# Hybrid transformer block: the down, attention-output and second-block output products as one 512-column and one 256-column matmul for each chunk of K

## The chip, the cores and the metric

The kernel runs on one core of one Trainium2 chip. Its metric is the device time of one execution in microseconds (us); lower is better. The kernel before was timed three times: 1444.11, 1445.13 and 1448.83 us, median 1445.13 us.

## The reference

The program is two blocks of two layers each, on 256 tokens (in the second block also 256 context tokens), width D = 1024, all in float32. The lines whose products the change touches are these:

```python
# first block, both layers
merged = gates[:, :, 0] * y_a + gates[:, :, 1] * y_b + gates[:, :, 2] * y_c
x = x + merged @ w_o                                  # 1024 x 1024
h = rmsnorm(x, norm_mlp)
return x + jnp.square(jax.nn.relu(h @ w_up)) @ w_down # 1024 x 4096, then 4096 x 1024
# second block, both layers: x (in its first layer also the context) gets
x = x + gate * (y @ w_out)                            # 1024 x 1024
```

The rest (the projections into queries, keys, values and gates, five kinds of attention and a long convolution, the norms) is as before.

## The kernel before, in words

**Layout.** Activations stand transposed: 128 features on the partitions, 256 tokens along the free dimension, so an activation of width 1024 is 8 chunks of 128x256. Weights come in tiles of 128x1024: for one block of 128 output features, 8 chunks of 128 input features.

**Precision.** Every large product is made of exact parts. A value v is split into hi, its rounding to the matmul's format (a copy on ScalarE, L291 for weights, L275 for activations), and lo = v - hi (a subtraction on VectorE, L292 and L276). For each chunk of K, `mm3` issues three matmuls into one accumulation: high weights by high activations (L332), high weights by low activations (L333), low weights by high activations (L334). The parts of an activation chunk lie side by side in one 128x512 tile (`pair`), except those of the MLP's hidden layer, which were two 128x512 tiles `uh` and `ul` for two chunks each. An output of 128 features by 256 tokens fills half of a PSUM bank (2 KB, 512 float32 columns).

**Weights.** `weights` loads a tile by a DMA on SyncE's queue into one of 5 raw buffers, and splits it into one of 3 hi and 3 lo buffers. So the hi copy of a tile waits until TensorE has finished the tile three before it, and TensorE has two tiles of work left when the copy starts.

**The first block's layer** ends with three stages: the output stage (8 outputs c of 64 matmul chunks in all, over the activations `mg`; VectorE adds each output to x[c], L753; `gx` makes the parts of the next stage's input h[c] from it, on ScalarE at L493 and on VectorE at L494; a square for the next norm goes to ScalarE, and is summed on GpSimd, L421), and two halves of the MLP, each an up stage (h times w_up, ReLU, square, split into u) and a down stage (16 chunks for each of 8 outputs; L785 multiplies by the norm's factor, L786 adds to x[c]). Between these, `fill` puts pieces of the second block that depend on nothing (conditioning products L840, spectra of the long convolution).

**The second block** has the same kind of output product three times: `project_out` for x and then for the context (8 outputs of 8 chunks; one VectorE operation for each output, L1154), and `project` in its last layer, in two halves of 8 outputs by 4 chunks (L1378), the very end of the program.

**Order.** The program is traced once, and a scheduler then sets the order of the instructions on each engine from the dependences and its own estimates. Each engine runs its list in order; waits between engines are semaphores. PSUM has three rotating banks for these products (`ps_mm`).

## Time and profile before

| | |
|---|---|
| runs | 1444.11, 1445.13, 1448.83 us |
| span of the profiled execution, first to last instruction | 1448.5 us |
| its own time | not listed apart from its span; of the three runs the slowest, 1448.83 us, lies 0.3 us above it |
| mean granted TensorE clock | 0.998 |
| TensorE matmuls | 1427.0 us busy, 99% of the span, 10528 of them |
| VectorE | 1048.7 us, 72% |
| ScalarE | 776.5 us, 54% |
| GpSimd | 108.4 us, 7% |
| DMA | 234.94 MB, 162 GB/s in the mean |

A matmul's recorded duration runs from its issue to the arrival of its last result, so consecutive matmuls overlap in the record; what one costs a stream of them is the distance between two starts. Busy times of VectorE overlap too, by some 0.08 us for each pair of instructions.

The stages that the change touches lie here (us from the span's start; the rows of their windows stand further below): first layer, output stage from 245.3 to 268.7, down stages from 320.8 to 374.5 and from 433.0 to 491.2; second layer, output stage from 724.5 to 748.0, down stages from 804.0 to 859.6 and from 912.0 to 959.2; second block, `project_out` for x from 1201.0 to 1224.6 and for the context from 1224.6 to 1248.5, `project` from 1420.9 to the end.

### The profile page before, as it was taken

To read this page: it belongs to the slowest core of one execution; us is meant where nothing else is said; L and a number is where in the kernel's file an instruction comes from. 1 tells how busy PE (TensorE), PEld (TensorE's weight loads), DVE (VectorE), ACT (ScalarE), POOL (GpSimd) and SP (SyncE) were. 2 spreads that over 40 slices of the span, in tenths; PEclk is the share of its full clock that TensorE was granted. 3 is DMA by queue.
4 is the path that set the end of the run, shared out by engine and by line. 5 is a ranking of instruction groups with operands and counts; after the bars stand their busy time and mean duration, and the time that the engine had idled before them with its cause. 6 is when DMAs were issued, how large, how long until landed. Compare 5 with 4: busy or idle time off the path is not lost. (4 is left out here: it accounts for less than half of the span.)

```text
span 1448.5 us, 26508 instructions
## 1 busy us (share of the span) xinstructions
PE 1427.0 (99%) x10528; PEld 1284.2 (89%) x10528; DVE 1048.7 (72%) x1878; ACT 776.5 (54%) x1407; POOL 108.4 (7%) x87
## 2 busy tenths in 40 slices
PE   8999999999999999999999999999999999999999
PEld 8988999998988998899998899997678889978788
DVE  5776768866657687666785567879877976986776
ACT  5455565543545435566454345557654335657664
POOL 3000000100002110000010002230001002200000
PEclk9999999999999999999999999999999999999999
DMA  7534555677786743455576766643114125521233
GB/s 264 171 107 142 164 161 172 210 245 243 236 266 210 261 149 118 138 167 159 173 218 223 241 221 201 196 160 127 37 63 141 45 85 177 171 96 48 74 95 110
DMA packets 73864, 234.94 MB, mean 162 GB/s; under 512 B 8875, under 2 KB 11532, under 8 KB 73740
## 3 DMA queue, kind: packets, MB, share of 16 engines
q1 hardware_dynamic: 71868, 231.65, 49.9%
q8 instruction: 83, 1.36, 0.4%
q10 hardware_dynamic: 1872, 1.59, 0.3%
q14 instruction: 41, 0.34, 0.1%
HBM read 229.54 MB, written 3.67 MB: 161 GB/s over the span
## 5 line engine op out<-in xcount | busy, mean ns | idle before, releaser
L291 ACT CAST hi<-raw 128x1024 fp32r<-128x1024 f32 (+2 forms) x378 | 380.7, 1009 | 398.8 <-PE ps_mm L333 226.5
L292 DVE TENSOR_TENSOR lo<-raw,hi 128x1024 fp32r<-128x1024 f32 (+2 forms) x367 | 436.8, 1191 | 216.7 <-ACT hi L291 202.7
L332 PE MATMUL ps_mm<-h,hi 128*128 128x256 f32 (+1 forms) x1712 | 521.2, 305 | 3.2 <-ACT hi L291 2.1
L334 PE MATMUL ps_mm<-h,lo 128*128 128x256 f32 (+1 forms) x1712 | 511.8, 299 | 5.1 <-DVE lo L292 5.1
L333 PE MATMUL ps_mm<-h,hi 128*128 128x256 f32 (+1 forms) x1712 | 510.8, 298 | 0.6 <-DVE h L494 0.3
L332 PEld LDWEIGHTS ps_mm<-h,hi 128*128 128x128 f32 x1712 | 328.1, 192 | 37.4 <-issue 22.3
L334 PEld LDWEIGHTS ps_mm<-h,lo 128*128 128x128 f32 x1712 | 328.1, 192 | 16.8 <-DVE lo L292 6.5
L333 PEld LDWEIGHTS ps_mm<-h,hi 128*128 128x128 f32 x1712 | 328.3, 192 | 10.1 <-DVE h L494 1.3
L332 PE MATMUL ps_mm<-uh,hi 128*128 128x256 f32 x512 | 147.5, 288 | 0.3 <-ACT uh L275 0.3
L333 PE MATMUL ps_mm<-ul,hi 128*128 128x256 f32 x512 | 145.3, 284 | 1.3 <-DVE ul L276 1.3
L334 PE MATMUL ps_mm<-uh,lo 128*128 128x256 f32 x512 | 144.8, 283 | 0.0
L332 PEld LDWEIGHTS ps_mm<-uh,hi 128*128 128x128 f32 x512 | 98.1, 192 | 14.4 <-issue 10.4
L421 POOL TENSOR_TENSOR acc<-acc,sq 128x256 f32<-128x256 f32 x54 | 59.3, 1101 | 647.3 <-ACT sq L417 646.6
L333 PEld LDWEIGHTS ps_mm<-ul,hi 128*128 128x128 f32 x512 | 98.1, 192 | 3.3 <-DVE ul L276 2.7
L334 PEld LDWEIGHTS ps_mm<-uh,lo 128*128 128x128 f32 x512 | 98.1, 192 | 0.0
L332 PE MATMUL ps_mm<-hi,h 128*128 128x384 f32 (+1 forms) x192 | 62.6, 326 | 0.0
L334 PE MATMUL ps_mm<-hi,h 128*128 128x384 f32 (+1 forms) x192 | 61.2, 319 | 0.0
L333 PE MATMUL ps_mm<-lo,h 128*128 128x384 f32 (+1 forms) x192 | 61.2, 319 | 0.0
L332 PE MATMUL ps_mm<-y,hi 128*128 128x256 f32 x192 | 54.6, 285 | 0.0
L334 PE MATMUL ps_mm<-y,lo 128*128 128x256 f32 x192 | 54.4, 284 | 0.0
L333 PE MATMUL ps_mm<-y,hi 128*128 128x256 f32 x192 | 54.3, 283 | 0.0
L395 ACT ACTIVATE p<-ps_s,mn 128x256 f32<-128x256 f32 (+1 forms) x64 | 33.8, 529 | 24.8 <-DVE mn L1099 12.3
(334 smaller groups left out, 2336.5 us busy)
## 6 DMA issues: line engine op xcount, KB each, us to landing
raw<-wu SPq DMA_DIRECT2D x64, 512.0 KB, 4.4
raw<-wd SPq DMA_DIRECT2D x64, 512.0 KB, 4.5
raw<-wg SPq DMA_DIRECT2D x48, 512.0 KB, 3.6
raw<-wo SPq DMA_DIRECT2D x48, 512.0 KB, 3.5
raw<-wada SPq DMA_DIRECT2D x48, 512.0 KB, 4.6
raw<-wqk SPq DMA_DIRECT2D x46, 512.0 KB, 4.4
raw<-w2e SPq DMA_DIRECT2D x32, 512.0 KB, 3.6
raw<-wv SPq DMA_DIRECT2D x32, 384.0 KB, 3.1
```

The lines of the kernel that those rows point to most:

```text
L291: self.nc.scalar.copy(hi[:, s], raw[:, s])
L292: (self.nc.gpsimd if pool else self.nc.vector).tensor_sub(lo[:, s], raw[:, s], hi[:, s])
L332: mm(out, wh, xh, start=start, stop=False)
L333: mm(out, wh, xl, start=False, stop=False)
L334: mm(out, wl, xh, start=False, stop=stop)
L395: self.last_exp = self.nc.scalar.activation(*args, **kw)
L421: nc.gpsimd.tensor_add(self.sum, self.sum, sq)
```

## The change

For the down products, the product with w_o and the second block's output products, `fm` gives way to `fm2`. For each chunk of K it issues two matmuls in place of three. The first has the high weights as its stationary operand and the whole 128x512 tile as its moving operand, high and low activations side by side, and writes a whole bank: the left half holds high by high, the right half high by low. The second adds low weights by high activations to the left half. The two halves of a bank are two partial sums of the same output, and are added by whoever reads the bank.

That reading changes as follows. In the output stage x[c] gets two additions in place of one. In `project_out` and `project` there are two scalar_tensor_tensor in place of one. In the first down half ScalarE copies the right half into a new tile `down`, and VectorE adds the left half; multiplication by the norm's factor and the addition to x[c] are gone there. In the second down half VectorE does four operations (right half, left half, multiply, add to x[c]) where it did two. The hidden layer's u is split in pieces of 256 columns in place of 512, so that the parts of a chunk lie side by side. The product of `oT` with the three branch matrices, the up product and all input projections keep their three matmuls.

```diff
+class _Pair(tuple):
+    def __new__(cls, parts, both):
+        self = super().__new__(cls, parts)
+        self.both = both
+        return self
...
-        return t[:, :T], t[:, T:]
+        return _Pair((t[:, :T], t[:, T:]), t)
...
+    def fm2(self, *args):
+        _run(self.fmg2(*args))
+    def fmg2(self, out, w, at, acts, start=True, stop=True):
+        hi, lo = w
+        n = len(acts)
+        mm = self.nc.tensor.matmul
+        for c in range(n):
+            s = slice((at + c) * P, (at + c + 1) * P)
+            mm(out, hi[:, s], acts[c].both, start=start and c == 0, stop=False)
+            mm(out[:, :T], lo[:, s], acts[c][0], start=False, stop=stop and c == n - 1)
+            if c % 4 == 3:
+                yield
...
-                hi, lo = k.pair("mg")
-                k.split(hi, lo, m[:, f * T:(f + 1) * T])
-                mg.append((hi, lo))
+                mg.append(k.pair("mg"))
+                k.split(*mg[-1], m[:, f * T:(f + 1) * T])
...
         early = []
         for c in range(2):
             early.append((k.psum(), next(wo)))
-            k.fm(early[c][0][:, :T], early[c][1], 0, mg[:6], True, False)
+            k.fm2(*early[c], 0, mg[:6], True, False)
         split_mg(m)
         for c in range(NCH):
             if c < 2:
                 p, w = early[c]
-                k.fm(p[:, :T], w, 6, mg[6:], False, True)
+                k.fm2(p, w, 6, mg[6:], False, True)
             else:
                 p = k.psum()
-                k.fm(p[:, :T], next(wo), 0, mg)
-            nc.vector.tensor_add(x[c], p[:, :T], x[c])
+                k.fm2(p, next(wo), 0, mg)
+            for i in range(2):
+                nc.vector.tensor_add(x[c], p[:, i * T:(i + 1) * T], x[c])
             h.append(gx(c, 2 * l + 1))
             acc.add(c, x[c])
         rs2 = None
+        down = [k.u("dn") for _ in range(4)]
         for hf in range(2):
             u = []
             for b in range(8 * hf, 8 * hf + 8):
...
                 if fill:
                     fill(l, 1)
-                r, uh, ul = k.t2("r"), k.u("uh", F32R, "v"), k.u("ul", F32R, "v")
+                r = k.t2("r")
                 nc.scalar.activation(r, p, AF.Relu)
                 nc.vector.tensor_mul(r, r, r)
-                k.split(uh, ul, r)
                 for f in range(2):
-                    s = slice(f * T, (f + 1) * T)
-                    u.append((uh[:, s], ul[:, s]))
+                    u.append(k.pair("u", "v"))
+                    k.split(*u[-1], r[:, f * T:(f + 1) * T])
             if hf:
                 h = []
                 if l == layers[-1]:
...
             for c in range(NCH):
                 p = k.psum()
                 for q in range(2):
-                    k.fm(p[:, :T], k.weights(ins["wd"][l, 2 * hf + q, c]), 0, u[8 * q:8 * q + 8], q == 0, q == 1)
-                t = k.t1("dn")
-                nc.vector.tensor_mul(t, p[:, :T], rs2)
-                nc.vector.tensor_add(x[c], x[c], t)
+                    k.fm2(p, k.weights(ins["wd"][l, 2 * hf + q, c]), 0, u[8 * q:8 * q + 8], q == 0, q == 1)
+                t = down[c // 2][:, c % 2 * T:c % 2 * T + T]
+                if hf == 0:
+                    nc.scalar.copy(t, p[:, T:])
+                else:
+                    nc.vector.tensor_add(t, p[:, T:], t)
+                nc.vector.tensor_add(t, p[:, :T], t)
+                if hf:
+                    nc.vector.tensor_mul(t, t, rs2)
+                    nc.vector.tensor_add(x[c], x[c], t)
                 if fill:
                     fill(l, 1)
                 if hf:
...
-        hi, lo = k.pair("y")
-        k.split(hi, lo, y)
-        out.append((hi, lo))
+        out.append(k.pair("y"))
+        k.split(*out[-1], y)
     def project_out(y, j, xx):
         for c in range(NCH):
             p = k.psum()
-            k.fm(p[:, :T], k.weights(ins["wo2"][0, c]), 0, y)
-            nc.vector.scalar_tensor_tensor(xx[c], p[:, :T], adc(0, 2, c, j), xx[c], op0=ALU.mult, op1=ALU.add)
+            k.fm2(p, k.weights(ins["wo2"][0, c]), 0, y)
+            for i in range(2):
+                nc.vector.scalar_tensor_tensor(xx[c], p[:, i * T:(i + 1) * T], adc(0, 2, c, j), xx[c], op0=ALU.mult, op1=ALU.add)
...
         for c in range(at, at + 4):
             gated(os_[c], sg[c], y)
         out = {}
         for c, a, b in [(c, a, b) for a, b in ((0, 3), (3, 4)) for c in range(2)] + [(c, 0, 4) for c in range(2, NCH)]:
             if a == 0:
                 out[c] = k.psum(), k.weights(ins["wo2"][1, c, :, at * P:(at + 4) * P], 4 * P)
             p, w = out[c]
-            _run(k.fmg(p[:, :T], w, a, y[a:b], a == 0, b == 4))
+            k.fm2(p, w, a, y[a:b], a == 0, b == 4)
             yield
             if b == 4:
-                nc.vector.scalar_tensor_tensor(x[c], p[:, :T], adc(1, 2, c, 0), x[c], op0=ALU.mult, op1=ALU.add)
+                for i in range(2):
+                    nc.vector.scalar_tensor_tensor(x[c], p[:, i * T:(i + 1) * T], adc(1, 2, c, 0), x[c], op0=ALU.mult, op1=ALU.add)
```

The line numbers of the changed program differ from those of before: L275 is L285 there, L292 is L301, L494 is L518, L753 is L777, L1378 is L1409, and `fm2`'s two matmuls are L368 and L369.

On TensorE, the first output of the first down stage (the numbers behind the names are those of the buffers). Before, after the last matmul of the up stage:

```order
L334 MATMUL ps_mm_3795<-h_3239,lo_3829 128x256
L332 MATMUL ps_mm_3865<-uh_3341,hi_3868 128x256
L333 MATMUL ps_mm_3865<-ul_3342,hi_3868 128x256
L334 MATMUL ps_mm_3865<-uh_3341,lo_3869 128x256
...
L332 MATMUL ps_mm_3865<-uh_3415,hi_3868 128x256
L333 MATMUL ps_mm_3865<-ul_3416,hi_3868 128x256
```

And in the changed kernel:

```order
L343 MATMUL ps_mm_3757<-h_3183,lo_3791 128x256
L368 MATMUL ps_mm_3829<-u_3291,hi_3832 128x512
L369 MATMUL ps_mm_3829<-u_3291,lo_3833 128x256
L368 MATMUL ps_mm_3829<-u_3294,hi_3832 128x512
L369 MATMUL ps_mm_3829<-u_3294,lo_3833 128x256
L368 MATMUL ps_mm_3829<-u_3367,hi_3832 128x512
```

The matmul of L333 is gone; that of L332 is twice as wide, and needs both parts of its chunk where it needed the high one.

On VectorE, the end of the first layer's output stage (x5_97 to x7_99 are the residual's chunks 5 to 7, h the parts of the up stage's input, lo the low part of a weight tile). Before:

```order
L753 TENSOR_TENSOR x5_97<-ps_mm_3137,x5_97 128x256
L292 TENSOR_TENSOR lo_3248<-raw_3245,hi_3247 128x1024
L494 SCALAR_TENSOR_TENSOR h_3169<-x5_97,g1_90,h_3169 128x256
L753 TENSOR_TENSOR x6_98<-ps_mm_3175,x6_98 128x256
L292 TENSOR_TENSOR lo_3278<-raw_3275,hi_3277 128x1024
L494 SCALAR_TENSOR_TENSOR h_3207<-x6_98,g1_90,h_3207 128x256
L753 TENSOR_TENSOR x7_99<-ps_mm_3213,x7_99 128x256
L292 TENSOR_TENSOR lo_3351<-raw_3348,hi_3350 128x1024
L494 SCALAR_TENSOR_TENSOR h_3239<-x7_99,g1_90,h_3239 128x256
```

And in the changed kernel:

```order
L777 TENSOR_TENSOR x5_97<-ps_mm_3102,x5_97 128x256 x2
L301 TENSOR_TENSOR lo_3196<-raw_3193,hi_3195 128x1024
L518 SCALAR_TENSOR_TENSOR h_3096<-x4_96,g1_90,h_3096 128x256
L518 SCALAR_TENSOR_TENSOR h_3127<-x5_97,g1_90,h_3127 128x256
L777 TENSOR_TENSOR x6_98<-ps_mm_3133,x6_98 128x256 x2
L301 TENSOR_TENSOR lo_3226<-raw_3223,hi_3225 128x1024
L518 SCALAR_TENSOR_TENSOR h_3158<-x6_98,g1_90,h_3158 128x256
L777 TENSOR_TENSOR x7_99<-ps_mm_3164,x7_99 128x256 x2
L301 TENSOR_TENSOR lo_3301<-raw_3298,hi_3300 128x1024
```

The second addition to x[c] stands ahead of a weight tile's subtraction, and the subtraction that makes h[c] comes behind both, as before.

On VectorE, the last outputs of the program. Before:

```order
L1378 SCALAR_TENSOR_TENSOR x3_95<-ps_mm_16877,adaT_2617,x3_95 128x256
L292 TENSOR_TENSOR lo_16941<-raw_16938,hi_16940 128x512
L1378 SCALAR_TENSOR_TENSOR x4_96<-ps_mm_16897,adaT_2617,x4_96 128x256
L292 TENSOR_TENSOR lo_16961<-raw_16958,hi_16960 128x512
L1378 SCALAR_TENSOR_TENSOR x5_97<-ps_mm_16917,adaT_2617,x5_97 128x256
L1378 SCALAR_TENSOR_TENSOR x6_98<-ps_mm_16937,adaT_2617,x6_98 128x256
L1378 SCALAR_TENSOR_TENSOR x7_99<-ps_mm_16957,adaT_2617,x7_99 128x256
```

And in the changed kernel:

```order
L301 TENSOR_TENSOR lo_16235<-raw_16232,hi_16234 128x512
L1409 SCALAR_TENSOR_TENSOR x3_95<-ps_mm_16180,adaT_2617,x3_95 128x256
L1409 SCALAR_TENSOR_TENSOR x4_96<-ps_mm_16197,adaT_2617,x4_96 128x256
L301 TENSOR_TENSOR lo_16252<-raw_16249,hi_16251 128x512
L1409 SCALAR_TENSOR_TENSOR x4_96<-ps_mm_16197,adaT_2617,x4_96 128x256
L1409 SCALAR_TENSOR_TENSOR x5_97<-ps_mm_16214,adaT_2617,x5_97 128x256 x2
L1409 SCALAR_TENSOR_TENSOR x6_98<-ps_mm_16231,adaT_2617,x6_98 128x256 x2
L1409 SCALAR_TENSOR_TENSOR x7_99<-ps_mm_16248,adaT_2617,x7_99 128x256 x2
```

Each output has two operations, most of them apart by a weight tile's subtraction, the last three side by side.

## Rows read from the trace of the kernel before

**Rows 1.** Page, part 1: busy us (share) and instructions of each engine.
```profile
PE 1427.0 (99%) x10528; PEld 1284.2 (89%) x10528; DVE 1048.7 (72%) x1878; ACT 776.5 (54%) x1407; POOL 108.4 (7%) x87
```

**Rows 2.** Groups of TensorE instructions, shapes apart: busy us, mean ns, idle before.
```profile
L333 PE MATMUL ps_mm<-ul,hi 128*128 128x256 f32 x512 | 145.3, 284 | 1.3 <-DVE ul L276 1.3
L333 PE MATMUL ps_mm<-mg,hi 128*128 128x256 f32 x128 | 36.1, 283 | 0.0
L333 PE MATMUL ps_mm<-y,hi 128*128 128x256 f32 x192 | 54.3, 283 | 0.0
```

**Rows 3.** Timeline of TensorE, down stage: start us, us, instruction, count.
```profile
490.05 0.28 PE L332 MATMUL ps_mm<-uh,hi 128*128 128x256 f32 x1
...
491.37 0.28 PE L334 MATMUL ps_mm<-uh,lo 128*128 128x256 f32 x1
```

**Rows 4.** Timeline of TensorE, an input projection with 512 columns.
```profile
1100.81 0.39 PE L332 MATMUL ps_mm<-h,hi 128*128 128x512 f32 x1
...
1102.85 0.39 PE L332 MATMUL ps_mm<-h,hi 128*128 128x512 f32 x1
```

**Rows 5.** Busy time by stage: PE, PEld, DVE, ACT, POOL, clock, DMA share, GB/s.
```profile
245.30:268.70 23.40, 23.22 (x194) 23.02 (x193) 21.40 (x30) 14.01 (x24) 5.09 (x6) 1.00 0.66 200
724.50:748.00 23.50, 23.50 (x196) 23.37 (x195) 21.14 (x29) 14.16 (x24) 4.98 (x6) 1.00 0.65 198
320.80:374.50 53.70, 53.13 (x423) 47.38 (x422) 34.58 (x63) 20.09 (x22) 0.00 (x0) 1.00 0.72 241
433.00:491.20 58.20, 57.08 (x439) 50.12 (x439) 43.35 (x62) 29.51 (x44) 12.93 (x11) 1.00 0.69 232
1201.00:1224.60 23.60, 23.60 (x194) 23.18 (x192) 15.19 (x21) 13.28 (x20) 8.18 (x6) 1.00 0.63 200
1224.60:1248.50 23.90, 23.90 (x196) 23.74 (x196) 21.67 (x35) 15.66 (x26) 8.14 (x6) 1.00 0.58 184
374.80:433.00 58.20, 55.85 (x424) 49.12 (x422) 33.02 (x36) 26.73 (x34) 2.61 (x2) 0.97 0.77 250
```

**Rows 6.** Timeline of VectorE, first layer's output stage; idle before in brackets.
```profile
251.97 0.42 DVE L753 TENSOR_TENSOR x<-ps_mm,x 128x256 f32<-128x256 f32 x1 [0.17 <-PE ps_mm L334]
...
261.37 1.23 DVE L292 TENSOR_TENSOR lo<-raw,hi 128x1024 fp32r<-128x1024 f32 x1 [0.27 <-ACT hi L291]
...
264.20 1.23 DVE L292 TENSOR_TENSOR lo<-raw,hi 128x1024 fp32r<-128x1024 f32 x1 [0.40 <-ACT hi L291]
...
267.09 1.23 DVE L292 TENSOR_TENSOR lo<-raw,hi 128x1024 fp32r<-128x1024 f32 x1 [0.45 <-ACT hi L291]
...
269.12 0.41 DVE L753 TENSOR_TENSOR x<-ps_mm,x 128x256 f32<-128x256 f32 x1
269.97 1.23 DVE L292 TENSOR_TENSOR lo<-raw,hi 128x1024 fp32r<-128x1024 f32 x1 [0.44 <-ACT hi L291]
271.11 0.48 DVE L494 SCALAR_TENSOR_TENSOR h<-x,g,h 128x256 fp32r<-128x256 f32 x1
```

**Rows 7.** Timeline of VectorE: two operations of which the second needs the first.
```profile
1227.59 0.42 DVE L372 SCALAR_TENSOR_TENSOR nt<-ps_n,rstd 128x256 f32<-128x256 f32 x1 [0.84 <-ACT rstd L371]
1228.05 0.43 DVE L373 SCALAR_TENSOR_TENSOR nt<-nt,rstd 128x256 f32<-128x256 f32 x1
```

**Rows 8.** Timeline of TensorE, where the up stage reaches the last chunk of h.
```profile
271.69 0.47 PE L333 MATMUL ps_mm<-h,hi 128*128 128x256 f32 x1
```

**Rows 9.** Waits from 1420 us to the end: us in total, times, longest.
```profile
DVE x L1378 <- PE ps_mm L334: 4.4, 8, 1.3
```

**Rows 10.** Timeline of VectorE, the last output of the program.
```profile
1445.03 0.48 DVE L1378 SCALAR_TENSOR_TENSOR x<-ps_mm,adaT,x 128x256 f32<-128x256 f32 x1 [0.95 <-PE ps_mm L334]
```

**Rows 11.** Timeline of VectorE, the end of the first layer.
```profile
491.69 0.43 DVE L785 TENSOR_TENSOR dn<-ps_mm,rstd 128x256 f32<-128x256 f32 x1 [0.55 <-PE ps_mm L334]
...
493.84 0.48 DVE L494 SCALAR_TENSOR_TENSOR h<-x,g,h 128x256 fp32r<-128x256 f32 x1
```

**Rows 12.** Waits of TensorE from 300 to 860 us.
```profile
PE ps_mm L333 <- DVE ul L276: 1.3, 2, 0.7
```

## The prediction

> **What bounds the kernel now.** I read the page's busy times first. TensorE's matmuls fill 99% of the span, VectorE 72%, ScalarE 54% [rows 1]: the reader is to see that a change pays if it shortens TensorE's stream and delays nothing that TensorE waits for. The groups of TensorE instructions with shapes kept apart come next, for the number of chunks that the change touches: 512 in the down stages, 128 in the output stages, 192 in the second block's outputs, 832 in all, with nearly no idle time before them [rows 2]. What a matmul costs in a stream is the distance of two starts, so the timeline of TensorE comes third: eleven steps of 256 columns take 491.37 - 490.05 = 1.32 us, 0.120 us each [rows 3], nine of 512 columns 1102.85 - 1100.81 = 2.04 us, 0.227 us each [rows 4]. 256 more columns cost 0.107 us, one column per cycle of 2.4 GHz, at a granted clock of 1.00; so some 0.013 us of every matmul goes with the instruction and not with its columns. Last come the windows by stage: TensorE is full in all that the change touches, but VectorE is not equally free in them. In the down stages it is busy 34.58 of 53.70 us and 43.35 of 58.20; in the output stages 21.40 of 23.40 and 21.14 of 23.50, in the context's output stage 21.67 of 23.90 [rows 5]. The changed kernel reads every bank twice, and in the last three that work meets an engine that is nearly full. The argument is about this.
>
> **TensorE's gain.** A chunk takes 3 x 0.120 = 0.360 us now, and 0.227 + 0.120 = 0.347 after, if a start after a 512-column matmul follows as in rows 4 and one after a 256-column matmul as in rows 3. Nothing in the trace alternates the two with new weights each time. The bounds: 0.360 us, no gain, if the wide one hides nothing, and 0.333 us (0.227 and the bare 0.107), 0.027 gained, if only one start in two had its fixed part. I take the sum of the two rows, since both hold for streams with new weights at each matmul: 0.0133 us x 832 = 11.1 us, of which 6.8 in the down stages, 1.7 in the output stages, 2.6 in the second block's outputs (0.85 for each 64 chunks).
>
> The Trainium skill, "TensorE: Matmul & The Clock Gate", section "Wait — 56ns, not 53.3ns?", gives a warm start-to-start of the columns at 2.4 GHz and about 2.5 ns. By that, 832 matmuls less are 2.1 us and not 11.1. The trace does not agree, at 256 columns or at 512, so the sum keeps the rows.
>
> **Down stages.** The gain is kept, -6.8 us. In the first half ScalarE takes over a copy from a bank and VectorE loses one operation of two. In the second half VectorE gets 2 x 8 more, at 0.40 to 0.46 us some 7 us, in a stage with 43.35 busy of 58.20 [rows 5]: covered. If that cover fails it costs up to 7.
>
> **Output stages, two.** After the last `mg` VectorE is nearly without a pause: its recorded waits are 0.17, 0.27, 0.40, 0.45 and 0.44 us, 1.73 in all [rows 6]. Eight second additions come to it. One costs 0.33 to 0.46 us, the latter where it stands right behind the first and needs its result, as the pair at 1227.59 and 1228.05 shows [rows 7]; 0.40 in the mean, 3.2 us. So the end of its list comes 3.2 - 1.7 = 1.5 us later. What is at this end? The low part of h's last chunk, at 271.11 to 271.59 [rows 6], and TensorE reaches the matmul that reads it at 271.69 [rows 8], without slack. The time by which TensorE comes there earlier is lost as well: the stage ends 1.5 us later than now, not 0.85 earlier. Bounds: -0.85 (all hidden) and +3.2 (no pause usable). Two stages: +3.0 us.
>
> **Second block.** For x, VectorE is busy 15.19 of 23.60 us [rows 5]: -0.85 is kept. For the context, 21.67 us and 8 x 0.40 = 3.2 make 24.9 in a stage of 23.9: the gain of 0.85 goes, and as 35 records overlap by 0.08 us each, no more than that: 0 (bounds -0.85 and +2). The last stage has two halves of 8 outputs, each with a weight subtraction of half the width of those in rows 6 (half of 1.23, 0.6 us) and now two operations of 0.40 us, 1.4 in all, against 4 x 0.347 = 1.39 of TensorE: VectorE becomes the bound. It gets 16 x 0.40 = 6.4 us of work, and its waits for TensorE there are 4.4 us [rows 9], of which the last, 0.95 before 1445.03 [rows 10], can be filled only if it runs behind, which it then does. 6.4 - 4.4 = +2.0 us, all at the end of the program. Bounds: +0.4 - 0.85 (only the last output's second operation shows, the gain kept) and +6.4.
>
> **Between the layers.** The next layer's h[7] needs four operations in a chain after the last down product in place of two: 2 x 0.46 = 0.9 us. Now it is ready at 493.84 + 0.48 = 494.32, 2.63 us after the 491.69 at which the first of them begins [rows 11], which is seven chunks of TensorE work (2.5 us), so nothing hides it: +0.9 (bounds 0 and +2, if a weight subtraction of 1.23 comes to stand in the chain). The second layer's end feeds x only to norms that the context's work covers.
>
> **Into the down stages.** TensorE waits there for the last low part of u, 1.3 us in two waits [rows 12]. u is split in pieces of 256 columns now, so the first of the two chunks is ready half an operation earlier on two engines (0.2 to 0.3 us each); against that a chunk's first matmul now needs both parts, 0.12 us more. I take -0.8 for all four transitions (bounds -1.3 and +0.5).
>
> **Sum.** -6.8 + 3.0 - 0.85 + 0 + 2.0 + 0.9 - 0.8 = -2.5 us. It is made in the profiled execution, whose span of 1448.5 us lies at the upper edge of the runs, 1444.11 to 1448.83; nothing in the sum scales with that, so I subtract it from the median: 1445.13 - 2.5 = 1442.6 us. About 0.3% (4.3 us) is what a measurement of this kernel can tell from no change, so this is no change that can be told.
>
> **The rivals.**
> - VectorE's additions are hidden. For it: five of the additions in an output stage can be placed between independent operations, and the order may find pauses that I count as lost. Against: the zero slack of rows 6 and 8. Then all 11.1 us are gained, with +0.9 and -0.8: 1434.1 us; with half of it, 1438.4.
> - VectorE's list becomes the stage: only half of its pauses can be used, since a pause while it waits for a weight copy comes before the work that would fill it. Output stages 2 x (3.2 - 0.9) = 4.6, end 6.4 - 2.2 = 4.2, context 1.7, layers 0.9: 11.4 - 6.8 - 0.85 = +3.8; and where TensorE then stands still for over 2 us, its clock may fall to half: in the stage with the longest waits, 374.8 to 433.0, the granted clock is 0.97 of full in the mean [rows 5], which over 58.2 us is 3.5 us at 1.2 GHz, 1.7 us lost. With one such fall 1445.1 + 3.8 + 1.7 = 1450.6 us. It decides from the point at which VectorE is over 2 us behind at the end of an output stage.
> - The change doesn't do what it says: the pair of a wide and a narrow matmul takes the 0.360 us of the upper bound. All else stays: +3.0 + 2.0 + 0.9 - 0.8 = +5.1, 1450.2 us. Against it: rows 3 and 4 both follow their columns.
> - The order of the second block's attention, which the scheduler sets anew behind the change, is better or worse by some us; no row prices that. It moves any case, by 2 us either way as I take it.
>
> **How the numbers follow.** Forecast 0.52, with its own range of 1439.5 to 1446 (bounds of its terms); hidden additions 0.26; VectorE as the stage 0.12; no gain on TensorE 0.05; a worse attention alone 0.05. Faster by over 0.3%: 0.11 of the forecast's 0.52 and 0.23 of the hidden case, 0.34. Slower by over 0.3%: 0.08 and 0.03 of the third and fourth, 0.11. Within: 0.55. The range of 8 in 10 goes from the middle of the hidden case to just short of the slow cases: 1436.5 to 1449.
>
> **What would show it.** Starts of 0.227 and 0.120 us in turn in the down stages, and these stages 1.7 us shorter each, show the gain; 0.120 after a wide one and 0.24 before it would show the bound. In the output stages VectorE without pauses and a wait of TensorE of 1.5 to 2.5 us for the low part of h show the price; no such wait, the first rival. In the last 24 us VectorE without waits for TensorE, and the last result over 1 us behind the last matmul. I am wrong if the time is under 1439.5 (cover that I did not see) or over 1446, and wrong in the mechanism if the down stages do not get shorter.

## The result, and the profile after

| | before | changed |
|---|---|---|
| runs, median | 1445.58 us (4 runs, 1444.11 to 1448.83) | 1456.18 us (4 runs, 1453.41 to 1459.29) |
| ratio, 95% interval | 1 | 1.0063 (1.0041 to 1.0086) |
| span of the profiled execution | 1448.5 us | 1455.2 us |

The change makes the kernel 0.63% slower, about 9 us by the ratio (the medians differ by 10.6). The forecast was 1442.6 us with an upper end of 1449.0. The two profiled executions differ by 6.7 us only: in all other runs the time lies some 1.8 us above the span, so the profiled execution of before would be one of some 1450 us (an estimate from that), slower than its four timed runs. The first part of the page, to be laid beside [rows 1], shows TensorE's matmuls 1.5 us less busy and VectorE 25 us more:

```profile
PE 1425.5 (98%) x9696; PEld 1239.1 (85%) x9696; DVE 1073.8 (74%) x1974; ACT 783.2 (54%) x1455; POOL 103.6 (7%) x87
```

The groups of TensorE's new matmuls, shapes apart (count | busy us, mean ns | idle before, releaser), answer to [rows 2]. There was no idle time before a `y` matmul; now there are 3.2 us:

```profile
L368 PE MATMUL ps_mm<-u,hi 128*128 128x512 f32 x512 | 183.6, 401 | 1.3 <-DVE u L285 1.3
L368 PE MATMUL ps_mm<-y,hi 128*128 128x512 f32 x192 | 68.5, 399 | 1.7 <-DVE x L1409 1.3 <-DVE y L285 0.4
L369 PE MATMUL ps_mm<-y,lo 128*128 128x256 f32 x192 | 54.0, 285 | 1.5 <-DVE lo L301 1.3
L369 PE MATMUL ps_mm<-mg,lo 128*128 128x256 f32 x128 | 35.2, 280 | 0.2 <-DVE lo L301 0.2
```

Wide and narrow matmuls do alternate as forecast. On the timeline of TensorE, in the fourth down stage, 113 chunks lie between these two starts: 956.33 - 917.15 = 39.18 us, 0.347 each, against 0.360 for three narrow ones [rows 3]. In the other three a chunk takes about 0.347 or about 0.357 us, by turns, 0.351 to 0.353 in the mean. So the wide matmul gives 7 to 13 ns a chunk:

```profile
917.15 0.28 PE L369 MATMUL ps_mm<-u,lo 128*128 128x256 f32 x1
...
956.33 0.28 PE L369 MATMUL ps_mm<-u,lo 128*128 128x256 f32 x1
```

The time by stage (columns as in [rows 5]; a window goes from the first or last product of a stage to that of the next) shows where it is gone. The first layer's output stage is 0.7 us shorter (22.66 against 23.36 between the same products), but the up stage behind it takes 53.59 for 52.22. The down stages take 52.60, 57.26, 53.73 and 45.46 for 53.75, 58.29, 55.44 and 46.86: -5.3 us. The three last windows lose: from the last down product to the second block's output 245.31 for 241.89, from there to `project` 175.26 for 172.56, and `project` 30.53 for 27.46:

```profile
246.08:268.74 22.66, 22.43 (x129) 19.27 (x128) 21.61 (x35) 13.40 (x22) 5.03 (x5) 1.00 0.64 202
268.74:322.33 53.59, 52.75 (x425) 47.57 (x424) 40.58 (x71) 27.03 (x43) 1.27 (x2) 1.00 0.69 232
956.33:1201.64 245.31, 240.31 (x1354) 191.98 (x1353) 196.73 (x387) 126.06 (x267) 13.50 (x7) 0.99 0.25 85
1249.31:1424.57 175.26, 171.86 (x1196) 142.14 (x1194) 133.14 (x345) 114.52 (x307) 1.06 (x1) 1.00 0.26 88
1424.57:1455.10 30.53, 24.17 (x128) 19.43 (x128) 25.11 (x56) 9.53 (x18) 0.00 (x0) 1.00 0.34 112
```

**Behind the output stage.** VectorE (timeline; it answers to [rows 6]) now has no pause in the stage from 252.30 on. The two additions to x[7] end at 271.60, a weight subtraction stands behind them, and the low part of h[7] is begun at 272.65. That is 1.5 us later than before on the clock of the trace, but the stage itself starts 0.8 us later in this execution: counted from the stage's first product it is 0.8 us later (26.6 against 25.8):

```profile
270.73 0.87 DVE L777 TENSOR_TENSOR x<-ps_mm,x 128x256 f32<-128x256 f32 x2
271.52 1.22 DVE L301 TENSOR_TENSOR lo<-raw,hi 128x1024 fp32r<-128x1024 f32 x1
272.65 0.48 DVE L518 SCALAR_TENSOR_TENSOR h<-x,g,h 128x256 fp32r<-128x256 f32 x1
```

TensorE (timeline; [rows 8] before) waits for both parts:

```profile
272.19 0.39 PE L341 MATMUL ps_mm<-h,hi 128*128 128x256 f32 x1 [0.67 <-ACT h L517]
...
273.18 0.38 PE L342 MATMUL ps_mm<-h,hi 128*128 128x256 f32 x1 [0.17 <-DVE h L518]
```

**The end of the second layer.** The last x of the first block is complete 3.3 us behind the start of TensorE's last down product (956.33 to 959.62), where it was 1.2 (959.10 to 960.31): four operations and a weight subtraction stand behind that product where two operations stood. Between VectorE's rows at 957.10 and 958.75 lies that subtraction:

```profile
956.64 0.42 DVE L812 TENSOR_TENSOR dn<-ps_mm,dn 128x256 f32<-128x256 f32 x1 [0.54 <-PE ps_mm L369]
957.10 0.42 DVE L813 TENSOR_TENSOR dn<-ps_mm,dn 128x256 f32<-128x256 f32 x1
957.60 1.22 DVE L301 TENSOR_TENSOR lo<-raw,hi 128x1024 fp32r<-128x1024 f32 x1
958.75 0.42 DVE L815 TENSOR_TENSOR dn<-dn,rstd 128x256 f32<-128x256 f32 x1
959.20 0.42 DVE L816 TENSOR_TENSOR x<-x,dn 128x256 f32<-128x256 f32 x1
```

TensorE runs through the context's work and then stands still twice (its waits from 956 to 1000 us of the changed kernel), and behind each of the two its granted clock falls to 1.2 GHz for a time: the mean is 0.79 and 0.81 of full in the two windows.

```profile
PE ps_n L1097 <- ACT vf L1092: 2.1, 1, 2.1
PE ps_mm L341 <- DVE qr L1070: 1.9, 1, 1.9
```

```profile
971.00:979.00 8.00, 5.87 (x35) 5.49 (x34) 7.13 (x17) 6.68 (x15) 0.00 (x0) 0.79 0.37 132
979.00:988.00 9.00, 6.95 (x32) 4.88 (x31) 7.06 (x12) 5.26 (x10) 0.00 (x0) 0.81 0.32 117
```

The kernel before had two waits there as well, of 2.0 and 1.3 us, and a clock of 1.00 in both halves of that stretch:

```profile
PE ps_n L1036 <- DVE qn L372: 2.0, 1, 2.0
PE ps_n L1067 <- ACT vf L1062: 1.3, 1, 1.3
```

```profile
960.00:975.00 15.00, 13.67 (x102) 12.71 (x101) 12.19 (x20) 8.70 (x17) 4.94 (x2) 1.00 0.32 105
975.00:990.00 15.00, 13.01 (x97) 11.52 (x95) 13.84 (x24) 10.82 (x18) 0.85 (x1) 1.00 0.53 172
```

The first wait, for the copy `vf`, is the longer one now. The product that waits starts 17.4 us behind the last down product, 14.2 before (973.68 and 973.33 in the two traces): 3.1 us later, of which TensorE fills 2.3 with work that the new order puts ahead of it. Two things make it late: x, by 2.1 us, and VectorE's meetings with GpSimd in the chain behind x, by 1.6 us (last section); the rest of the chain is 0.6 us quicker.

**Second block.** The context's last product starts at 1249.31, but VectorE, which has no pause in that stage, comes to its second operation only at 1252.23, 2.9 us later (0.3 before). TensorE waits 0.96 us for the context's norm, that is for GpSimd's sum of the squares of the first seven outputs, and 0.8 us behind it for the next queries. In `project` VectorE's waits for TensorE are 1.5 us in all (4.4 before [rows 9]), and TensorE now waits for VectorE:

```profile
DVE x L1409 <- PE ps_mm L369: 1.5, 2, 1.1
PE ps_mm L368 <- DVE x L1409: 1.3, 1, 1.3
PE ps_mm L369 <- DVE lo L301: 1.1, 2, 0.6
PE ps_mm L368 <- DVE y L285: 0.4, 1, 0.4
```

### The profile page after: what moved, and what is told of

The parts are those of the page before. It is cut to its first block, busy times and chain, and to the rows that moved or that the text cites. A ratio compares the mean times of both kernels' runs of the same rounds, so it can differ in the third digit from the quotient of the medians.

```text
span 1455.2 us, 24988 instructions
## 1 busy us (share of the span) xinstructions
PE 1425.5 (98%) x9696; PEld 1239.1 (85%) x9696; DVE 1073.8 (74%) x1974; ACT 783.2 (54%) x1455; POOL 103.6 (7%) x87
## 5 line engine op out<-in xcount | busy, mean ns | idle before, releaser
L301 DVE TENSOR_TENSOR lo<-raw,hi 128x1024 fp32r<-128x1024 f32 (+2 forms) x367 | 437.1, 1193 | 211.3 <-ACT hi L300 201.0
L343 PEld LDWEIGHTS ps_mm<-h,lo 128*128 128x128 f32 x1712 | 329.1, 192 | 17.4 <-DVE lo L301 7.5
L368 PE MATMUL ps_mm<-u,hi 128*128 128x512 f32 x512 | 183.6, 401 | 1.3 <-DVE u L285 1.3
L369 PE MATMUL ps_mm<-u,lo 128*128 128x256 f32 x512 | 143.7, 281 | 0.0
L368 PEld LDWEIGHTS ps_mm<-u,hi 128*128 128x128 f32 x512 | 96.1, 188 | 38.6 <-issue 9.6
L445 POOL TENSOR_TENSOR acc<-acc,sq 128x256 f32<-128x256 f32 x54 | 54.6, 1015 | 647.8 <-ACT sq L441 647.0
L369 PEld LDWEIGHTS ps_mm<-u,lo 128*128 128x128 f32 x512 | 96.7, 189 | 0.5 <-DVE dn L812 0.2
L368 PE MATMUL ps_mm<-y,hi 128*128 128x512 f32 x192 | 68.5, 399 | 1.7 <-DVE x L1409 1.3
L369 PE MATMUL ps_mm<-y,lo 128*128 128x256 f32 x192 | 54.0, 285 | 1.5 <-DVE lo L301 1.3
L368 PEld LDWEIGHTS ps_mm<-y,hi 128*128 128x128 f32 x192 | 36.0, 188 | 11.1 <-ACT y L284 1.6
L368 PE MATMUL ps_mm<-mg,hi 128*128 128x512 f32 x128 | 44.8, 397 | 0.0
L301 POOL TENSOR_TENSOR lo<-raw,hi 128x1024 fp32r<-128x1024 f32 x11 | 27.6, 2511 | 197.8 <-ACT hi L300 197.8
```

The costliest lines, as they stand in the source:

```text
L301: (self.nc.gpsimd if pool else self.nc.vector).tensor_sub(lo[:, s], raw[:, s], hi[:, s])
L343: mm(out, wl, xh, start=False, stop=stop)
L368: mm(out, hi[:, s], acts[c].both, start=start and c == 0, stop=False)
L369: mm(out[:, :T], lo[:, s], acts[c][0], start=False, stop=stop and c == n - 1)
L445: nc.gpsimd.tensor_add(self.sum, self.sum, sq)
```

## The experiments

Ratios are to the kernel before, measured on the same chip; five alternating rounds each. Theories: **A**, VectorE's second reads cost where VectorE is full; **B**, the new order of the second block's attention costs; **C**, the late end of the first block costs, by waits and falls of the clock; **D**, late weights behind the first layer's output stage take time back; **E**, scatter.

### The change in parts

`mg_only`, `down_only` and `y_only` keep the wide matmul in one kind of product and give the other two back, as these lines do for `mg`:

```diff
-                k.fm2(p, next(wo), 0, mg)
-            for i in range(2):
-                nc.vector.tensor_add(x[c], p[:, i * T:(i + 1) * T], x[c])
+                k.fm(p[:, :T], next(wo), 0, mg)
+            nc.vector.tensor_add(x[c], p[:, :T], x[c])
```

> Only the output stages (mg, 128 chunks) have the wide matmul and the two reads; down products and second block as before, and TensorE's order in the second block is the one of before. Theory A (the second reads are the loss, where VectorE is full): the stages and the up stages behind them together lose; in the changed kernel stage plus following up stage were 76.25 us against 75.58 and 80.41 against 79.71, +1.4 in both layers, of which TensorE's gain of 128 x 0.010 = 1.3 is already taken off. So +1.4 us, ratio 1.001, and a wait of TensorE for the low part of h of 0.6 to 0.8 us behind each stage. Theory B (the loss is the new order of the second block's attention): the same +1.4 at most, and 959 to 1201 us takes 241.9 us as before. Forecast as put on record: +3.0.

> Only the down products (512 chunks) have the wide matmul, u in pieces of 256 columns, the right half through ScalarE or VectorE; output stages and second-block outputs as before. The scheduler sets the start of the second block's attention in the new order here too. TensorE's gain is 512 x 0.010 = 5.1 us in the four down stages. Theory A: that gain stays, ratio 0.9965 to 0.997 (-4.5 to -5 us), since no stage here has a full VectorE. Theory B: the gain is given back between the last down product and project_out: that stretch, 241.9 us before, takes 244 to 245.5 us, with waits of over 2 us near 971 and 981 and a fall of the clock; ratio 0.999 to 1.0.

> Only the second block's outputs (192 chunks) have the wide matmul and two reads. The order up to the first of them is the one of before, behind it a new one. TensorE's gain is 1.9 us. Theory A: x's output -0.6, the context's output +1 (a wait of TensorE for the norm behind it), the last stage +3 as in the changed kernel (30.5 us from its first product to the end against 27.5): +3 us in all, ratio 1.002. Theory B: beside that the stretch between the context's output and the last stage grows by 2.7 us (175.3 against 172.6): +6 us, ratio 1.004.

| wide matmul in | ratio, interval |
|---|---|
| output stages (`mg_only`) | 1.0038 (1.0024 to 1.0052) |
| down products (`down_only`) | 0.9971 (0.9957 to 0.9985) |
| second-block outputs (`y_only`) | 1.0043 (1.0029 to 1.0056) |

The parts add up to 1.0052. Only the down products gain. `y_only` loses 6.2 us, as much as its trace locates: x's 64 chunks -0.6, the context's +0.9, the stretch to `project` +2.7, `project` to the end +3.1. The waits in that stretch are VectorE's lag behind the context (1.0 us for the norm's sum, 0.8 for the next queries, 0.4 at the start of `project`), so A holds and B is not needed there. `down_only` shows both falls of the clock near 971 and 981 us, and 245.4 us in place of 241.9 for the stretch behind the last down product, as B expected, while its ratio is the one that A expected; whether the order or the late x makes the falls, it doesn't tell. `mg_only` loses 5.5 us, of which its trace locates 1.4 (75.6 to 76.2 us and 79.7 to 80.4): my expectation was too low. That trace is of the fastest of its twelve runs (1449.31 us, the others 1451.29 to 1459.37), so most of the loss isn't in it.

### The wide matmul taken apart

```diff
-            mm(out, hi[:, s], acts[c].both, start=start and c == 0, stop=False)
+            mm(out[:, :T], hi[:, s], acts[c][0], start=start and c == 0, stop=False)
+            mm(out[:, T:], hi[:, s], acts[c][1], start=False, stop=False)
```

> The changed kernel with the wide matmul taken apart into two of 256 columns (high by high into the left half, high by low into the right half): same reads, same splitting, no gain on TensorE beyond what the order gives. Theory that TensorE gains 0.010 us a chunk: TensorE's stream is 8.3 us longer than in the changed kernel, less where TensorE waits for VectorE anyway; by A some 5 us slower than the changed kernel (ratio to before 1.010), the four down stages as long as before (53.8, 58.3, 55.4, 46.9 us), the last stage 0.3 us longer than in the changed kernel or the same. If instead it is as fast as the changed kernel (1.006), the wide matmul gives nothing.

1.0060 (1.0040 to 1.0080), the same as the changed kernel: a miss of the total. By stage the gain is there: the down stages take 53.7, 58.2, 55.3 and 47.3 us, as before the change, 5.5 us more than with the wide matmul. But output and up stage take 76.36 and 80.50 us, 0.1 from the changed kernel, and the last stage 30.28 against 30.53. There TensorE's shape changes nothing, since VectorE sets the time. Its profile gives 2.1 of the 5.5 us back in the first layer's second up stage (55.96 against 58.03 us; weights come late there, see below) and 0.9 ahead of the first stage that the change touches. Whether the runs do so in the mean, two profiles can't tell.

### The end of the first block

`down_tail` is `down_only` with three narrow matmuls for the last output of a second half, and its first half's part added to x early; `after_tail` is the same edit in the changed kernel.

```diff
+                    wd = k.weights(ins["wd"][l, 2 * hf + q, c])
+                    if last and hf:
+                        k.fm(p[:, :T], wd, 0, u[8 * q:8 * q + 8], q == 0, q == 1)
+                    else:
+                        k.fm2(p, wd, 0, u[8 * q:8 * q + 8], q == 0, q == 1)
...
+                if last and hf:
+                    nc.vector.tensor_mul(t, p[:, :T], rs2)
```

> The kernel with the wide matmul in the down products alone, but the last output of each second half (c = 7) has three narrow matmuls, one multiplication and one addition behind them as before; its first half's part is added to x early. Theory C (the four operations behind the last product, with a weight subtraction among them, make the norms of the second block late; TensorE, which comes earlier, then waits 2.29 and 2.37 us near 968 and 978, and the clock falls twice there, 1.6 us each): x is ready 1.2 us behind the last product as before, not 3.3; the two waits go to 1.5 and 2.1 us or less, the falls in that stretch become rare, ratio 0.9955 to 0.9965. Rival (the waits and falls come with the new order of the attention's start, which stays): 2.3 us twice and two falls as in the kernel that it is made from, ratio 0.997.

> The changed kernel, all of it, but the last output of each second half of the MLP with three narrow matmuls and two operations behind it, as in the down-only kernel with that tail. Theory C (of the 9 to 10 us some 3 are two more falls of the clock near 974 and 984 us, made by the late norms): waits of 1.5 and 2.1 us there in place of 2.3 and 2.3, mean granted clock 0.998 in place of 0.996, ratio 1.004. Rival (the falls come from elsewhere): clock 0.996, ratio 1.006.

`down_tail`: 0.9960 (0.9944 to 0.9977). `after_tail`: 1.0046 (1.0032 to 1.0060). In both TensorE's waits go back to what they were; of `down_tail`, on TensorE's timeline:

```profile
970.75 0.44 PE L1105 MATMUL ps_n<-im,vf 128*128 128x128 f32 x2 [1.32 <-ACT vf L1100]
...
978.75 1.12 PE L1074 MATMUL ps_n<-qsq,bo 128*128 128x512 f32 x2 [1.98 <-DVE qn L396]
```

The clock stays at 1.00 there in `down_tail` and falls once in `after_tail` (stretch 243.39 us); the mean over the runs is 0.998 in both (0.9975 in `down_only`; 0.995 or 0.996 in three of the changed kernel's four, 0.945 in the fourth). The waits go as C said. The runs gain 0.1 to 0.2% by the edit, inside the intervals. With the shorter tail the scheduler also went back to the order of before in that stretch, and the chain behind x to one meeting with GpSimd in place of two, so B and C can't be told apart there; one edit cures all. What a fall costs is shown by two profiles with the same order of instructions: the stretch takes 241.89 us before, and 243.46 in `y_only`, whose clock falls once behind the wait at 977: 1.6 us. A fall is not certain. Of the 16 profiles of all runs whose two waits there are 1.3 and 2.0 us, seven have one fall in the stretch and nine none; the four whose first wait is 2.1 us (the changed kernel, `narrow`, `down_only`, `raw6_after`) have two each.

### Where VectorE sets the time

`ends` keeps the wide matmul but for the last outputs of each stage and all of `project`; `y_pool2` is `y_only` with every second low part in `project` made on GpSimd:

```diff
-                out[c] = k.psum(), k.weights(ins["wo2"][1, c, :, at * P:(at + 4) * P], 4 * P)
+                out[c] = k.psum(), k.weights(ins["wo2"][1, c, :, at * P:(at + 4) * P], 4 * P, pool=c % 2 == 1)
```

> The changed kernel with the wide matmul kept wherever VectorE has time until the stage ends: down products but the last output of a second half, output stages but their last two outputs, x's output in the second block, the context's but its last two; the program's last stage (project) as before. Theory C and A (the loss is what the second reads put behind the last products of a stage and into the last stage): the wait behind an output stage (0.83 and 0.43 us) falls to under 0.5, stage and next up stage take 75.2 and 79.3 us (before 75.6 and 79.7), the end is as before (27.5 us), the wait for the context's norm 0.2 in place of 1.1; ratio 0.994 to 0.996. Rival (any second read in the output stages is paid in full, wherever it stands): each output stage still loses 0.7 us, ratio 0.997 to 0.999.

> The kernel with the wide matmul in the second block's outputs alone; in the program's last stage the low parts of every second weight tile are made on GpSimd (idle there) in place of VectorE. Theory A (VectorE is what the last stage waits for): it has 1.1 us an output in place of 1.4, against 1.40 of TensorE; the stretch from the first product to the end goes from 30.6 us to 27.0 to 28 (27.5 before), ratio 1.002 to 1.0025. Rival (TensorE waits there for banks or for ScalarE's weight copies, VectorE only ends last): 30 us or more as without it, ratio 1.004.

`y_pool2`: 1.0014 (0.9999 to 1.0028). The last stage, of `y_only` and then of `y_pool2`, in the columns of [rows 5]:

```profile
1422.01:1452.60 30.59, 24.20 (x128) 19.49 (x128) 25.13 (x56) 9.53 (x18) 0.00 (x0) 1.00 0.35 112
```

```profile
1423.87:1452.00 28.13, 23.67 (x128) 19.54 (x128) 22.25 (x49) 9.51 (x18) 9.89 (x7) 0.99 0.36 122
```

Seven subtractions fewer on VectorE give 2.5 us back: theory A, shown (28.13 us, where 27.0 to 28 was expected). `ends`: 0.9986 (0.9971 to 1.0002). The waits behind the output stages are gone, and stage plus up stage take 75.41 and 79.49 us, 0.2 less than before in both and 0.2 more than expected. So the rival, by which every second read is paid in full, doesn't hold in the stage, though the ratio lies in its range. The rest missed: the context's norm is still waited for 0.5 us and the queries behind it 0.6, and the runs are slower than those of `down_tail` by 0.26% (3.8 us; the intervals just overlap), of which the trace locates 1 us.

### What is lost behind the first layer's output stage

`mg_l0` and `mg_l1` are `mg_only` for one layer alone; nothing outside that stage differs from before in kind or order. `mg_l0_one_read` reads only the left half there.

```diff
-            for i in range(2 if l == 0 else 1):
+            for i in range(1):
```

> The wide matmul with two reads in the first layer's output stage alone (64 chunks); every other instruction stands as before. The stage and the up stage behind it lose 0.7 us in the trace of the kernel with both (22.67 + 53.57 against 23.36 + 52.22), for both layers 1.4; that kernel's runs are 5 us slower. Theory D (the rest is lost behind the first layer's stage, where weights come late and TensorE waits for transfers near 326, 406 and 485 us): this kernel is some 4 us slower, ratio 1.0025 to 1.003. Theory E (the rest is the scatter of runs, nothing more is lost): ratio 1.0005.

> The wide matmul with two reads in the second layer's output stage alone; every other instruction as before. No weights come late behind it. Theory D: only the 0.7 us that the trace shows, ratio 1.0005. Theory E: the same 1.0005 and equal to the first layer's. If this one is the slower, neither holds, and the loss lies in the stage or in the clock behind it.

> The wide matmul in the first layer's output stage alone, and the right half of each bank left unread (the product of high weights and low activations is left out of x there): TensorE's gain without VectorE's second reads. Theory A (the second reads are all of the loss): the stage and the up stage behind it take 74.9 us (75.6 before), no wait behind the stage, ratio 0.9995. Rival D (something behind the stage takes it back whatever is read: weights that come late, the clock): ratio 1.002 to 1.003 as with the reads, with the second down stage at 59.8 us (57.8 to 58.6 in the kernels that are the same as before there).

`mg_l0` 1.0034 (1.0022 to 1.0047), `mg_l1` 1.0014 (0.9999 to 1.0030), `mg_l0_one_read` 1.0033 (1.0016 to 1.0050). The last one was decisive. In its trace stage and up stage take 74.87 us as expected, 0.7 less than before and 1.3 less than with the reads (76.21), so the reads' price in the stage is 1.3 us. And its runs are as slow as with the reads: something behind the stage takes back more than TensorE gains, whoever reads. The trace doesn't hold that loss, for it is of the fastest of twelve runs (1445.91 us; they go up to 1458.06). The mean granted clock of its runs is 0.9968, against 0.9983 before.

In the stretch behind that stage ScalarE waits for weight transfers. A sixth buffer for weight tiles (and 34 activation buffers for 36) lets these start earlier:

```diff
-        t = self.wp.tile([P, 1024], F32, name="raw", tag="raw", bufs=5)
+        t = self.wp.tile([P, 1024], F32, name="raw", tag="raw", bufs=6)
```

> The kernel before with six buffers for weight tiles in place of five (and two fewer of the 36 activation buffers). Theory D (the stretch from 270 to 490 us is bound by late weights): the waits of ScalarE for weight transfers there, 32 us in sum, fall by half, TensorE's 2.9 us of standing still near 407 shrink, fewer falls of the clock, ratio 0.998 or lower. Rival (the transfers come when the queue lets them, not when a buffer is free): no change, 1.000.

> Six weight buffers, and the wide matmul in the first layer's output stage without the second reads (the product of high weights and low activations left out of x there). Theory D: with the transfers early nothing takes the 0.7 us back: as the kernel before with six buffers, or 0.0005 less. Rival (it is not the transfers): 0.003 more than that kernel, as it is with five.

> The same with the second reads. Theory D and A: 0.7 us (0.0005) more than the kernel before with six buffers, the part that the trace shows in the stage. Rival: 0.0034 more, as with five.

ScalarE's waits for weights from 270 to 490 us, of the kernel before, and of it with six buffers:

```profile
ACT hi L291 <- DMA raw<-wd: 17.0, 6, 3.9
ACT hi L291 <- DMA raw<-wu: 15.2, 6, 5.1
```

```profile
ACT hi L291 <- DMA raw<-wu: 2.4, 2, 1.4
ACT hi L291 <- DMA raw<-wd: 2.3, 1, 2.3
```

| | five buffers | six buffers |
|---|---|---|
| before | 1 | 0.9983 (0.9974 to 0.9992) |
| first layer's stage, one read | 1.0033 (1.0016 to 1.0050) | 0.9987 (0.9978 to 0.9996) |
| first layer's stage, two reads | 1.0034 (1.0022 to 1.0047) | 0.9996 (0.9986 to 1.0006) |

The first layer's second up stage, of the kernel before and of it with six buffers, in the columns of [rows 5]:

```profile
374.66:433.08 58.42, 56.07 (x425) 49.27 (x424) 33.02 (x36) 26.73 (x34) 2.61 (x2) 0.97 0.77 250
```

```profile
374.14:428.38 54.24, 54.24 (x425) 47.72 (x423) 32.92 (x36) 28.05 (x36) 2.60 (x2) 1.00 0.79 269
```

The 14 profiles with five buffers have 54.5 to 60.2 us there, the six with six buffers 54.2 each. The runs draw together too: those of the one-read kernel lie between 1445.91 and 1458.06 us with five buffers, between 1444.82 and 1447.77 with six. With the weights early the loss of the one-read kernel is gone, and what the reads add is 0.0009, as much as the 1.1 us that the stage shows (76.24 against 75.17 us), though the intervals overlap. D holds: where a stretch waits for transfers, a stage in front of it that ends 0.7 us earlier gains nothing; that it loses nearly 5 us is measured, but which transfer meets which in those runs no trace here shows. The sixth buffer isn't free of side effects: it also sets a new order between the two layers, where the stretch takes 235.6 us in place of 233.1.

### The whole change, and the best version, with six buffers

> The changed kernel with six buffers for weight tiles. What the traces locate: both output stages +1.4 us, the second block's outputs +6.1, the down stages -5.3, two falls of the clock near 974 and 984 +3.2: +5.4 us against the kernel before with six buffers (0.9983), so 1.002 against the kernel before with five. If late weights are no part of the changed kernel's loss, 1.0046 or more (1.0063 less the 0.0017 that the sixth buffer gives the kernel before).

> The best version so far (the wide matmul in the down products alone, the last output of each second half narrow) with six weight buffers. If the two gains add: 0.996 times the ratio of the kernel before with six buffers, 0.993 to 0.995. If the down stages' gain was already lost to late weights in part, more than that.

> The down-only kernel with the tail, and the wide matmul with two reads in the second block's output for x (64 chunks), where VectorE is busy 15.2 of 23.6 us. In the kernel with the second block's outputs alone x's 64 chunks took 22.45 in place of 23.02 us. Theory A (a second read costs nothing where VectorE has time): -0.6 us beside the one without, ratio 0.9955. Rival (it is paid by the norm that runs beside the context's output): 0.996 to 0.997.

> The down products with the narrow last output, x's output in the second block with the wide matmul and two reads, six weight buffers. Theory A (a second read is free where VectorE has time): 0.6 us less than without x's part (0.9957), 0.9953. Rival (paid in the norm beside the context's output): 0.996.

The last two give `project_out` for x the wide matmul beside the down products. Measured: `raw6_after` 1.0026 (1.0015 to 1.0038), `raw6_down_tail` 0.9957 (0.9944 to 0.9969), `down_x` 0.9971 (0.9957 to 0.9985), `raw6_down_x` 0.9957 (0.9944 to 0.9970). Against the kernel before with six buffers the changed kernel loses 0.0043, 6.2 us. So of its 9 us some 3 would be late weights; this is a difference of two ratios from different chips, and their intervals leave room for none. The gains of the narrow last output and of the sixth buffer don't add: 0.9957 with both, where 0.993 to 0.995 was expected, and 0.9960 without the buffer. x's part takes 0.5 us off its stage in the trace (46.87 us for both outputs, 47.39 before) and nothing that the runs can tell: 0.9971 with five buffers and 0.9957 with six, beside 0.9960 and 0.9957 without it. The best version, level with `raw6_down_x`, is `raw6_down_tail`: median 1441.91 us, beside 1447.62 for the kernel before on the same chip, 0.43% faster by the ratio.

## Why the prediction was wrong, point by point

With six buffers late weights hardly blur the stages, so the terms are compared in that pair of profiles, unless a row says otherwise.

| step of the prediction | forecast, us | measured, us |
|---|---|---|
| four down stages | -6.8 | -5.1 (53.21, 57.44, 54.50, 46.86 to 51.96, 56.03, 53.73, 45.22) |
| two output stages | +3.0 | +1.4 |
| second block, x | -0.85 | -0.5 |
| second block, context | 0 | +0.9, and +2.7 in the stretch behind it |
| last stage | +2.0 | +3.1 |
| between the layers | +0.9 | +0.3 (+0.8 with five buffers) |
| into the down stages | -0.8 | 0 (waits for u of 1.3 us before and after with five buffers, none in either with six) |
| second layer's end | 0 | +1.9 (two falls of the clock against one; +3.4 with five buffers, two against none) |
| late weights | not in the sum | about +3 by the ratios, inside their intervals |

Without the last row the measured terms make +4.7 us, or +6.3 with the two falls of the changed kernel set against none before; the runs of that pair differ by 6.2.

**TensorE's gain: right in kind.** The chunk costs 0.347 to 0.353 us in the mean of a stage, 0.347 was forecast, so 5.1 of the 6.8 us came; the rival without a gain is refuted by the down stages. The Trainium skill, "TensorE: Matmul & The Clock Gate", section "Wait — 56ns, not 53.3ns?", has 2.5 ns of fixed cost for a matmul; by it, as an estimate, the down stages would have gained 1.3 us, and they gained 5.1.

**Output stages: right in kind.** The end of VectorE's list came 0.8 us later, not 1.5, and the wait for h[7] came, 0.67 and 0.17 us where 1.5 to 2.5 was forecast, for VectorE found more of its pauses than I allowed.

**Second block: a wait left out, and mis-sized terms.** I took the context's term as 0, "as 35 records overlap by 0.08 us each", and let the stage's end be the end of the matter. It wasn't: an engine that is 2.9 us behind when TensorE is done is waited for by the next chain, here a norm whose sum needs the context's outputs. For the last stage I took all 4.4 us of VectorE's pauses as usable, and 1.5 us of them stayed. The rival "VectorE's list becomes the stage" had the mechanism, 1.7 and 4.2 us for context and end; 3.6 and 3.1 were measured.

**The second layer's end: the step that failed outright.** "The second layer's end feeds x only to norms that the context's work covers" is false: TensorE already stood still 1.3 and 2.0 us there before, so there was no cover; these waits are in the trace of the kernel before, and the prediction doesn't use them. x came 2.1 us later behind the last product, by the four operations and the subtraction between them, and the chain behind x met GpSimd once more. The first wait grew to 2.1 us, the second, 1.9 us, came at another product, and each was followed by a fall of the clock. The rival's "over 2 us" for such a fall is no limit: seven of 16 profiles have one behind the wait of 2.0 us.

**Late weights: not priced at all.** The window of 374.8 to 433.0 us in [rows 5] has a DMA share of 0.77 and a clock of 0.97; I read it as a place for clock falls and not as a stretch that sets its own time. With six buffers the same products take 54.24 us at a clock of 1.00, so 4.2 us of that profiled execution were late weights.

**Open:** why `narrow` is no slower than the changed kernel in its runs; the 2 to 3 us by which `ends` is slower, beside `down_tail`, than its trace says; what part of the second layer's end is the late x and what the new order and its meetings with GpSimd; and how a stage that ends 0.7 us earlier comes to cost nearly 5 us in a stretch with late weights.

## What to carry to other kernels

Work that is moved from TensorE to the engine that reads its banks is free only in stages where that engine both has time and isn't waited for at the end: ask for each stage how far behind the reader is when the last product is done, and who waits for that. A wide matmul for the bulk and the old form for the last outputs keeps the gain without the tail. Before pricing a shorter stage, look whether the next stretch waits for transfers; if it does, try a further buffer for the transfers first.

## What the runs showed of the hardware that was not expected

A fall of the granted clock cost 1.6 us in the stretch of 241.9 us, and runs of one and the same kernel differ along with it: of the kernel before, beside `mg_only`, those with a mean clock of 1.000 took 1445.1 to 1445.8 us and those with 0.996 took 1450.9 to 1451.7. How much of these 6 us is the clock and how much the waits ahead of its falls, the times don't show. So a change that adds waits of 2 us pays in the wait and, in some executions, in the clock behind it.

VectorE's operations with two SBUF operands were slowed beside GpSimd here. In the changed kernel three that begin the modulation took 3.33 us (VectorE's timeline), with a subtraction of GpSimd's beginning 0.14 us ahead of them; three of the same line took 1.28 without it. Another operation of that chain, at 962.78, took 1.43 us for 0.42 beside a subtraction of GpSimd's that runs from 961.55 to 963.94. Ahead of the first wait the changed kernel so loses 3.1 us in two such meetings, and the kernel before 1.5 us in one (966.33).

```profile
968.54 3.33 DVE L1005 SCALAR_TENSOR_TENSOR mt<-x,gg,rstd 128x256 f32<-128x256 f32 x3
```

```profile
968.40 2.40 POOL L301 TENSOR_TENSOR lo<-raw,hi 128x1024 fp32r<-128x1024 f32 x1 [4.47 <-ACT hi L300]
```

The other one, and the one of the kernel before:

```profile
962.78 1.43 DVE L397 SCALAR_TENSOR_TENSOR nt<-nt,rstd 128x256 f32<-128x256 f32 x1
```

```profile
966.33 1.88 DVE L372 SCALAR_TENSOR_TENSOR nt<-nv,rstd 128x256 f32<-128x256 f32 x1 [1.17 <-ACT rstd L371]
```

The additions from a bank, which have one SBUF operand, kept 0.48 us beside GpSimd's subtractions in `y_pool2`, which fits that the move to GpSimd paid there. The Trainium skill, "SBUF — State Buffer", section "Who interferes with whom", says both: a VectorE instruction with two SBUF inputs contends with a GpSimd instruction that reads SBUF, one with a single SBUF input outside the two-port modes doesn't. The trace agrees.
